# Moving the sums of the down projection's weights to another stage, and twelve additions to another engine, in a hybrid decoder layer

## The chip, the cores and the metric

The kernel runs on one core of one Trainium2 chip. The metric is the device time of one execution in microseconds; several runs are summed up by their median. The engines have short names in the profile: PE is TensorE's matrix products (PEld its weight loads), DVE is VectorE, ACT is ScalarE, POOL is GpSimd, SP is SyncE, which issues most of the transfers. Each engine takes its instructions from a queue of its own, in order: one that waits holds up those behind it.

## The reference

One layer of a hybrid decoder for 1024 tokens of width 1024, with 16 learned meta tokens in front:

```
hn = rmsnorm(h, mix_norm_g);  proj = hn @ w_in
o_sb  = stick_breaking_attention(8 heads of 64)
o_ssm = ssd_mixer(conv of 4 taps + silu, 16 heads of 64, state 128, gate, rmsnorm)
o_mla = mla_attention(8 heads of 64 + 32, low-rank q and kv)
h = h + concat(o_sb, o_ssm, o_mla) @ w_out
fn = rmsnorm(h, ffn_norm_g)
h = h + (silu(fn @ w_gate) * (fn @ w_up)) @ w_down        # width 2816
out = rmsnorm(h, final_norm_g)
```

All in float32. The kernel makes each product from three, by splitting each operand into a high part (rounded, fp32r) and a low remainder: high x high, low x high, high x low.

## The kernel before, in words

The stages follow one another in the program, and each is a block of pools: stick-breaking attention for four pairs of heads (with the convolution's dense products `conv_unit` and the next pair's projections between); the state-space chunks (`ssd_chunk`, nine of them) with the latent projections (`latent_units`, `latent`, `scaled_unit`); eight MLA heads (`mla_head`) followed in the program by the gate's products (`gate_units`) and the output projection (`out_rows`); the gate and up projections (`GateUp`); the down projection.

The order in which the instructions really stand in the queues is not the program's. The framework's scheduler puts each instruction into its engine's queue by its own model of time: those earlier in the program go first, but one that is further back is taken when its engine would be free, its inputs are there and its buffer is free. So dense products stand between the attention's steps.

A dense product takes its weights by `load_w`: a load into `wraw` (one buffer), ScalarE's cast to `whi`, POOL's remainder `wlo` (L136). TensorE's lines L147 to L149 are the three products.

The down projection, gate and up are done by a fast scheme with seven products in place of eight (Strassen in Winograd's form): of the 22 blocks of the inner width, 18 are taken as nine pairs (NS = 9). It needs sums of blocks of the weights. `down_sums(p, c)` makes those for `w_down`, pair p and column quarter c, 36 calls in all: two loads of 128 KB into a tile `wd` of 2 KB per partition (L694), four POOL operations of 128 x 128 (L696) and a store of 256 KB to `s_wsum` (L697), which the down projection reads from 1563 us on. In the kernel before, `wd` uses the buffers `vst` and `vsp` (tags of one buffer each, in pool `sbb`), which `load_value_steps` also uses for the values of the next pair of heads (loads at L408, POOL's L410 and L359). The calls stand in the loop over pairs of heads, three after each convolution unit. Other POOL work of that stage: `csig` (L496), `oTs` (L351); other loads and stores on SP: `s_osbl` (L353), `s_xs` (L497), `wraw` (L132).

POOL's work in the state-space chunks: `y` (L755), `Xd` (L802), `S` (L833), `y` plus `ea` (L825). SP's there: `bc` and `xs` (L751, L752), `lraw` (L859). In the MLA heads: POOL's `mlo` (L960), `V` (L359), and `gy` (L537), `grow` (L510) of the gate; SP's `st` (L956).

Memory: the pools concerned are stacked from the right edge of SBUF. The stick-breaking stage has sbq, sbv and sbb, with tiles for 107.4 KB per partition; the last tags that sbb holds are the buffers `oTh` and `oTl` (oTs). After it, `ga` (4.2 KB) stays, and above it `la` and `p2` (45.8 and 53.5 KB) for the state-space chunks and latents; these go, and `ml` and `mr` (44.2 and 57.3 KB) come for the MLA heads. `reuse_waits="tile"` lets a tile wait only for the tiles that lay at its place.

The down projection loops over the seven products (`product(i, banks, start)`) and in each over the nine pairs; `operands(i, p)` loads a weight block and a hidden block into `raw`, ScalarE casts (L1517), and the remainder is made in two halves, one by POOL and one by VectorE (both L1519). TensorE's products are L1529 to L1531. The first product is kept in four tiles `E1` (the tiles named grow and E in the profile), and later added to three quarters of the result `hT` (hF in the profile): twelve additions of 128 x 512 by the helper `add` (L1104), in the kernel before on POOL.

Of the kernel before, what the change touches and what calls it, by code (L numbers as in the profile page):

```python
# [11 lines left out]
F32 = mybir.dt.float32  # L12
# [3 lines left out]
ALU = mybir.AluOpType  # L16
# [19 lines left out]
NS = 9  # L36
# [23 lines left out]
def tile_hybrid_block(ctx: ExitStack, tc: tile.TileContext, a: dict):  # L60
    nc = tc.nc
    act, dve, pool, pe, sp = nc.scalar, nc.vector, nc.gpsimd, nc.tensor, nc.sync
# [24 lines left out]
    s_wsum = dram.tile([NS, 4, 128, 4, 128], F32, name="s_wsum")  # L87
# [29 lines left out]
    for e, (m, base) in enumerate(((sb_mask, -1), (mla_mask, 0))):  # L117
# [3 lines left out]
            out=full, in_=full, pattern=[[-1, 128]], compare_op=ALU.is_ge, fill=NEG,  # L121
# [139 lines left out]
    def normalise(i, row):  # L261
# [11 lines left out]
        out=tri, in_=tri, pattern=[[1, 128]], compare_op=ALU.is_ge, fill=0.0, base=0, channel_multiplier=-1  # L273
# [366 lines left out]
    for i, (q0, qn) in enumerate(((0, 256), (256, 384), (640, 384))):  # L640
# [3 lines left out]
        c0, n = CH_ALL[i]  # L644
# [8 lines left out]
    with ctx_sb as st:  # L653
        sbb = st.enter_context(tc.tile_pool(name="sbb", bufs=2, side="right", reuse_waits="tile"))
        sc = st.enter_context(tc.tile_pool(name="sc1", bufs=3, space=PSUM, reuse_waits="tile"))
        pvp = st.enter_context(tc.tile_pool(name="pv1", bufs=1, space=PSUM, reuse_waits="tile"))

        def sb_row(Qh, Kh, KSh, i):
            n_all = META + 128 * (i + 1)
            cm = sbb.tile([128, T], F32, tag="cm", bufs=4, name="cm")  # L660
            qs = Qh[:, 128 * i : 128 * (i + 1)]
            chunks = key_chunks(i)
            for c0, n in chunks[::-1]:
                ps = sc.tile([128, 512], F32, tag="sc", name="sc_ps")
# [14 lines left out]
        pms = meta_tiles(sbb)  # L679

        def sb_attend(p, proj, values):
            Q, K, KS = proj
            for h in range(2):
                for j in range(NQ // 2):
                    rows = [sb_row(Q[h], K[h], KS[h], 2 * j + e) for e in range(2)]
                    weighted_values(tp, pvp, sbb, j, rows, values[0], h, [x[p, 64 * h : 64 * (h + 1)] for x in (s_osbh, s_osbl)], pms[j % 2], values[1])

        def down_sums(p, c):

            w = sbb.tile([128, 5, 2, 64], F32, tag=("vst", "vsp")[c % 2], bufs=1, name="wd")  # L690
            w = w.rearrange("p b h d -> p (b h d)")[:, :512].rearrange("p (q n) -> p q n", q=4)
            for e in range(2):
                src = a["w_down"][2 * p + e].rearrange("p (h c n) -> p h c n", h=2, c=4)
                sp.dma_start(w[:, e::2], src[:, :, c])  # L694
            for out, x, y, op in ((2, 0, 2, ALU.subtract), (3, 3, 2, ALU.subtract), (0, 0, 3, ALU.add), (1, 1, 3, ALU.subtract)):
                pool.tensor_tensor(w[:, out], w[:, x], w[:, y], op=op)  # L696
            sp.dma_start(s_wsum[p, c], w)  # L697

        sums = [(p, c) for p in range(NS) for c in range(4)]
        values = load_value_steps(sbv, sbb, 0)  # L700
        step_sizes()
        convs = [8, 9, 10, 11, 0, 1, 2, 3, 4, 5, 6, 7]
        for p in range(4):
            sb_attend(p, proj, values)
            if p < 3:
                if p == 1:
                    sb_values(1, [load_w(a["w_sbv"][1, u]) for u in range(2)], range(9))
                proj, k_evac, q_evac = sb_project(p + 1)
                dense_fm(dpool, load_w(a["w_sbk"][p + 1]), KT, 128, hn_mov, CH_ALL, k_evac)
                dense_fm(dpool, load_w(a["w_sbq"][p + 1]), KT, 128, hn_real, CH_REAL, q_evac)  # L710
                values = load_value_steps(sbv, sbb, p + 1)
            for u in convs[3 * p : 3 * p + 3]:
                conv_unit(u)
                for x in sums[:3]:
                    down_sums(*x)
                del sums[:3]
    real = [(128 * b, 128) for b in range(NQ)]


# [221 lines left out]
    with ExitStack() as st:  # L941
        ml = st.enter_context(tc.tile_pool(name="ml", bufs=2, side="right", reuse_waits="tile"))
        mr = st.enter_context(tc.tile_pool(name="mr", bufs=2, side="right", reuse_waits="tile"))
        sc = st.enter_context(tc.tile_pool(name="sc4", bufs=3, space=PSUM, reuse_waits="tile"))
        pvp = st.enter_context(tc.tile_pool(name="pv4", bufs=1, space=PSUM, reuse_waits="tile"))

# [52 lines left out]
        def mla_head(c):  # L999
            nonlocal V  # L1000
            p, h = c // 2, c % 2
            if h == 0:
                V = load_values(mr, s_v, p, ml)
            proj = mla_load(c)
            inv = mr.tile([128, NQ], F32, tag="inv", bufs=2, name="inv")
            for j in range(NQ // 2):
                rows = [mla_row(proj, i, inv[:, i : i + 1]) for i in (2 * j, 2 * j + 1)]
                weighted_values(tp, pvp, mr, j, rows, V, h, s_omla[p, 64 * h : 64 * (h + 1)], pms[j % 2])

                if j == 1 and c == MLA_HEADS - 1:  # L1010
                    inverse_sums(c, inv, 0, NQ // 2)
            inverse_sums(c, inv, NQ // 2 if c == MLA_HEADS - 1 else 0, NQ)

        def inverse_sums(c, inv, i0, i1):
# [4 lines left out]
            dve.reciprocal(rows, pt[:n, 0:128])  # L1019
            sp.dma_start(s_inv[c, 128 * i0 : 128 * i1].rearrange("(i p) -> i p", p=128), rows)  # L1020

        V = None
        pms = meta_tiles(mr)
        for c in range(MLA_HEADS):
            mla_head(c)
        gate_r = gate_units()
        spread_row(grow, gate_r, real, CH_REAL)
        hn_stack.close()
# [74 lines left out]
    def add(out, x, y, eng=None):  # L1103
        (eng or dve).tensor_tensor(out, x, y, op=ALU.add)  # L1104
# [437 lines left out]
    gather(B, 4, lo)  # L1542
    for o in range(4):
        for ot, c in ((o, 1), (o + 4, 0), (o + 4, 1)):
            add(hT[ot][:, HALF[c]], hT[ot][:, HALF[c]], E1[o], pool)
    product(2, A, False)
    gather(A, 0, lo)
    product(5, B, False)
# [191 lines left out]
```

## Time and profile before

| what | us |
|---|---|
| median of 3 runs | 1823.75 (1821.61 to 1826.12) |
| the profiled execution's own time | 1822.58 |
| its span, first to last instruction | 1820.7 |
| TensorE busy | 1718.0 (94%), mean granted clock 0.975 |
| VectorE busy | 1101.7 (61%) |
| ScalarE busy | 849.5 (47%) |
| POOL busy | 932.1 (51%) |
| DMA | 227.08 MB, 125 GB/s on the mean |

The profile is of one execution. A row of "busy by stretch" gives the stretch from and to in us from the span's start, its length, then for each engine its busy time and its instructions in brackets, the granted TensorE clock as a share of full speed, the DMA engines' busy share and GB/s. A row of the waits reads "who waited <- for what: us in all, how often, longest". A row of a group reads "line engine operation output<-inputs shape xcount | busy us, mean ns of one | idle before it". A row of the timeline reads "start, us, engine, line ..." with the idle time before it and what ended it in square brackets. A matrix product's end is modelled, so rows of TensorE overlap; the distance between their starts is its pace.

### The profile page before, as it was taken

The numbers are of one execution on the slowest core, as the hardware profiler recorded it, in microseconds if no ns is written. First come the engines' busy times: TensorE is split into PE (matmuls) and PEld (weight loads), VectorE is DVE, ScalarE is ACT, GpSimd is POOL, SyncE is SP. The second block draws the span as 40 slices with busy tenths as digits, with TensorE's granted clock in tenths as the row PEclk, the third lists the DMA queues.
The fourth block names the chain that finished last, engine by engine and source line by source line (L and its number), as shares of the span: only waits on it lengthen the run. The fifth ranks groups of instructions, "written<-read, shape, count | busy, mean of one in ns | idle before, by whom it ended". The sixth has DMA issues, their size and how long they took to land.

```text
span 1820.7 us, 26880 instructions
## 1 busy us (share of the span) xinstructions
PE 1718.0 (94%) x9769; PEld 1504.6 (83%) x9769; DVE 1101.7 (61%) x1681; ACT 849.5 (47%) x1809; POOL 932.1 (51%) x743
## 2 busy tenths in 40 slices
PE   8959999979999988999999999899999999989997
PEld 7849998979998768998888877678888888868887
DVE  8687665657744563445675646986566676554434
ACT  7545564545557654667544423522222232343333
POOL 4446437665357646555321334655445445387643
PEclk9969999999999989999999999899999999999999
DMA  4223235443253456435631424132333322886502
GB/s 157 60 75 121 85 90 161 143 145 107 78 163 115 150 166 177 125 110 173 201 93 41 120 81 157 53 104 95 108 115 101 98 93 98 310 256 208 162 1 93
DMA packets 176456, 227.08 MB, mean 125 GB/s; under 512 B 25586, under 2 KB 121876, under 8 KB 176324
## 3 DMA queue, kind: packets, MB, share of 16 engines
q1 hardware_dynamic: 156928, 209.81, 36.7%
q10 hardware_dynamic: 19396, 15.56, 2.8%
q8 instruction: 77, 1.26, 0.3%
q14 instruction: 55, 0.45, 0.1%
HBM read 155.20 MB, written 70.12 MB: 124 GB/s over the span
## 4 chain that ended last, share of the span: by engine, by line
PE 63%; DVE 11%; POOL 7%; DMA 7%; ACT 6%; issue 5%; SPq 1%; ACTq 0%; POOLq 0%; DVEq 0%
PE d_ps L147 6%; PE b_ps L1315 6%; PE b_ps L1317 6%; PE b_ps L1316 6%; PE d_ps L148 6%; PE d_ps L149 6%; PE b_ps L1530 2%; PE b_ps L1531 2%; PE b_ps L1529 2%; POOL wd L696 2%; DMA wd<-in_w_down_dram 1%; PE ptg L322 1%; ACT L L796 1%; PE pv L301 1%; PE ptg L324 1%
## 5 line engine op out<-in xcount | busy, mean ns | idle before, releaser
L147 PE MATMUL d_ps<-hnh,whi 128*128 128x384 f32 (+6 forms) x744 | 248.7, 334 | 7.8 <-DVE cacc L491 5.4
L148 PE MATMUL d_ps<-hnh,wlo 128*128 128x384 f32 (+6 forms) x744 | 245.5, 330 | 2.1 <-POOL wlo L136 2.1
L149 PE MATMUL d_ps<-hnl,whi 128*128 128x384 f32 (+6 forms) x744 | 246.6, 331 | 0.0
L136 POOL TENSOR_TENSOR wlo<-wraw,whi 128x1024 fp32r<-128x1024 f32 (+1 forms) x57 | 136.5, 2395 | 185.1 <-ACT whi L134 166.1
L147 PEld LDWEIGHTS d_ps<-hnh,whi 128*128 128x128 f32 (+1 forms) x744 | 140.8, 189 | 12.7 <-issue 5.8
L148 PEld LDWEIGHTS d_ps<-hnh,wlo 128*128 128x128 f32 (+1 forms) x744 | 140.8, 189 | 5.5 <-POOL wlo L136 2.4
L149 PEld LDWEIGHTS d_ps<-hnl,whi 128*128 128x128 f32 (+1 forms) x744 | 140.8, 189 | 2.5 <-issue 0.3
L1315 PE MATMUL b_ps<-T,wh 128*128 128x512 f32 x352 | 138.2, 393 | 0.5 <-DVE u L1104 0.5
L1316 PE MATMUL b_ps<-T,wl 128*128 128x512 f32 x352 | 138.2, 393 | 0.0
L1317 PE MATMUL b_ps<-T,wh 128*128 128x512 f32 x352 | 137.7, 393 | 0.1
L308 DVE TENSOR_TENSOR pl<-ptg,ph 128x512 fp32r<-128x512 f32 (+1 forms) x160 | 99.3, 629 | 48.3 <-ACT ph L307 47.0
L1519 POOL TENSOR_TENSOR op<-raw,op 128x512 fp32r<-128x512 f32 x61 | 97.9, 1615 | 58.4 <-ACT op L1517 57.4
L1519 DVE TENSOR_TENSOR op<-raw,op 128x512 fp32r<-128x512 f32 x61 | 64.4, 1066 | 84.4 <-ACT op L1517 84.4
L674 DVE TENSOR_TENSOR_SCAN cm<-cm,zcol 128x144 f32<-128x144 f32 (+3 forms) x64 | 100.6, 1577 | 22.7 <-ACT cm L672 22.5
L1517 ACT CAST op<-raw 128x1024 fp32r<-128x1024 f32 x61 | 63.6, 1053 | 106.7 <-PE d_ps L1531 75.0
L696 POOL TENSOR_TENSOR wd<-wd 128x128 f32<-128x128 f32 x144 | 81.6, 581 | 61.3 <-DMA wd<-in_w_down_dram 58.2
L307 ACT CAST ph<-ptg 128x512 fp32r<-128x512 f32 (+1 forms) x160 | 84.8, 541 | 48.1 <-PE ptg L324 33.4
L1098 POOL TENSOR_TENSOR wlo<-raw,whi 128x1024 fp32r<-128x1024 f32 x18 | 45.5, 2528 | 96.6 <-ACT whi L1097 96.6
L491 DVE SCALAR_TENSOR_TENSOR cacc<-d_ps,cw,cacc 128x384 f32<-128x384 f32 (+3 forms) x108 | 61.8, 573 | 48.3 <-ACT cacc L484 46.3
L134 ACT CAST whi<-wraw 128x1024 fp32r<-128x1024 f32 (+1 forms) x57 | 58.8, 1032 | 48.2 <-PE d_ps L149 32.7
L1097 ACT CAST wh<-raw 128x512 fp32r<-128x512 f32 x88 | 52.8, 615 | 58.5 <-PE b_ps L1317 55.7
L1315 PEld LDWEIGHTS b_ps<-T,wh 128*128 128x128 f32 x352 | 66.1, 188 | 16.4 <-DVE u L1104 1.3
(443 smaller groups left out, 5311.2 us busy)
## 6 DMA issues: line engine op xcount, KB each, us to landing
s_hops<-gs SPq DMA_DIRECT2D x63, 256.0 KB, 2.0
raw<-s_hops SPq DMA_DIRECT2D x63, 256.0 KB, 5.0
raw<-in_w_gate_dram SPq DMA_DIRECT2D x22, 512.0 KB, 3.5
raw<-in_w_up_dram SPq DMA_DIRECT2D x22, 512.0 KB, 4.3
wd<-in_w_down_dram SPq DMA_DIRECT2D x72, 128.0 KB, 2.7
s_wsum<-wd SPq DMA_DIRECT2D x36, 256.0 KB, 2.6
raw<-s_wsum SPq DMA_DIRECT2D x36, 256.0 KB, 4.7
wraw<-in_w_o_dram SPq DMA_DIRECT2D x16, 512.0 KB, 4.4
```

The source lines that it names most:

```text
L136: pool.tensor_tensor(lo[:, :cols], raw[:, :cols], f32(hi[:, :cols]), op=ALU.subtract)
L147: pe.matmul(ps[:m, :n], wh, mh, start=(kt == 0), stop=False)
L148: pe.matmul(ps[:m, :n], wl, mh, start=False, stop=False)
L149: pe.matmul(ps[:m, :n], wh, ml, start=False, stop=(kt == nkt - 1))
L307: act.copy(ph[:, :n], pt[:, :n])
L308: dve.tensor_tensor(pl[:, :n], pt[:, :n], f32(ph[:, :n]), op=ALU.subtract)
L674: dve.tensor_tensor_scan(rev, rev, zcol.to_broadcast([128, n_all]), 1.0, ALU.mult, ALU.add)
L696: pool.tensor_tensor(w[:, out], w[:, x], w[:, y], op=op)
L1315: pe.matmul(banks[j], hi[:, ks], UH[u][k], start=start and k == 0, stop=False, skip_group_check=skip)
L1316: pe.matmul(banks[j], lo[:, ks], UH[u][k], start=False, stop=False, skip_group_check=skip)
L1317: pe.matmul(banks[j], hi[:, ks], UL[u][k], start=False, stop=stop and k == 3, skip_group_check=skip)
L1519: eng.tensor_tensor(lo[:, s], raw[:, s], f32(hi[:, s]), op=ALU.subtract)
```

## The change

`down_sums` and its list `sums` move from the stick-breaking stage's block to that of the MLA heads. Its tile gets a pool of its own, `wd`, with one buffer of 2 KB per partition, opened behind `ml` and `mr`. The calls stand behind the heads: six behind each of heads 1 to 6. And the twelve additions of `E1` lose the argument `pool`, so that `add` puts them on VectorE.

```
-        def down_sums(p, c):
-
-            w = sbb.tile([128, 5, 2, 64], F32, tag=("vst", "vsp")[c % 2], bufs=1, name="wd")
-            w = w.rearrange("p b h d -> p (b h d)")[:, :512].rearrange("p (q n) -> p q n", q=4)
...
-        sums = [(p, c) for p in range(NS) for c in range(4)]
...
             for u in convs[3 * p : 3 * p + 3]:
                 conv_unit(u)
-                for x in sums[:3]:
-                    down_sums(*x)
-                del sums[:3]
...
         mr = st.enter_context(tc.tile_pool(name="mr", bufs=2, side="right", reuse_waits="tile"))
+        wd = st.enter_context(tc.tile_pool(name="wd", bufs=1, side="right", reuse_waits="tile"))
...
+        def down_sums(p, c):
+
+            w = wd.tile([128, 4, 128], F32, tag="wd", bufs=1, name="wd")
+            for e in range(2):
+                src = a["w_down"][2 * p + e].rearrange("p (h c n) -> p h c n", h=2, c=4)
+                sp.dma_start(w[:, e::2], src[:, :, c])
+            for out, x, y, op in ((2, 0, 2, ALU.subtract), (3, 3, 2, ALU.subtract), (0, 0, 3, ALU.add), (1, 1, 3, ALU.subtract)):
+                pool.tensor_tensor(w[:, out], w[:, x], w[:, y], op=op)
+            sp.dma_start(s_wsum[p, c], w)
...
+        sums = [(p, c) for p in range(NS) for c in range(4)]
         for c in range(MLA_HEADS):
             mla_head(c)
+            for x in sums[:6] if c > 0 else ():
+                down_sums(*x)
+                sums.remove(x)
...
     for o in range(4):
         for ot, c in ((o, 1), (o + 4, 0), (o + 4, 1)):
-            add(hT[ot][:, HALF[c]], hT[ot][:, HALF[c]], E1[o], pool)
+            add(hT[ot][:, HALF[c]], hT[ot][:, HALF[c]], E1[o])
```

More of the change, by code (lines that the diff above doesn't have):

```diff
@@ L686, in sb_attend @@
                     weighted_values(tp, pvp, sbb, j, rows, values[0], h, [x[p, 64 * h : 64 * (h + 1)] for x in (s_osbh, s_osbl)], pms[j % 2], values[1])
-        def down_sums(p, c):
-            w = sbb.tile([128, 5, 2, 64], F32, tag=("vst", "vsp")[c % 2], bufs=1, name="wd")
-            w = w.rearrange("p b h d -> p (b h d)")[:, :512].rearrange("p (q n) -> p q n", q=4)
[L692 to L697, printed above, removed]
-        sums = [(p, c) for p in range(NS) for c in range(4)]
         values = load_value_steps(sbv, sbb, 0)
```

## The prediction

> **What bounds the kernel now.** I read the page's busy times first, then busy time by stretch, then the waits and the chain inside the stretches that the change touches.
>
> ```profile
> PE 1718.0 (94%) x9769; PEld 1504.6 (83%) x9769; DVE 1101.7 (61%) x1681; ACT 849.5 (47%) x1809; POOL 932.1 (51%) x743
> ...
> L696 POOL TENSOR_TENSOR wd<-wd 128x128 f32<-128x128 f32 x144 | 81.6, 581 | 61.3 <-DMA wd<-in_w_down_dram 58.2
> ```
>
> ```profile
> core 0: us, PE busy (x) PEld busy (x) DVE busy (x) ACT busy (x) POOL busy (x), PEclk, DMA share, GB/s
> ...
> 512.00:700.00 188.00, 177.07 (x1268) 150.09 (x1267) 104.24 (x180) 112.71 (x316) 111.50 (x79) 0.97 0.49 152
> 700.00:830.00 130.00, 124.21 (x858) 120.33 (x857) 57.14 (x139) 88.67 (x218) 77.12 (x61) 1.00 0.45 130
> ...
> 140.00:260.00 120.00, 119.97 (x880) 115.95 (x880) 83.15 (x113) 69.91 (x165) 52.74 (x57) 1.00 0.31 93
> 300.00:420.00 120.00, 104.27 (x664) 98.86 (x663) 68.94 (x103) 56.47 (x128) 85.25 (x114) 0.97 0.48 150
> 1598.00:1640.00 42.00, 35.58 (x143) 28.50 (x142) 24.40 (x21) 19.18 (x22) 39.52 (x26) 0.92 0.79 249
> ```
>
> ```profile
> 360.00:400.00 40.00, 29.42 (x182) 27.07 (x181) 20.91 (x30) 17.04 (x39) 26.52 (x38) 0.95 0.43 135
> ```
>
> TensorE bounds the program: 94% busy, 102.7 us idle in the whole span, so an edit is worth only the idle (and the slowed clock) that it takes away or puts in. The rows show where. In 140 to 260, in the stick-breaking stage, TensorE never stops. In 300 to 420, the same stage with most of the sums in it, it idles 15.7 us and its clock is at 0.97; 360 to 400 alone holds 10.6 us of that. In 1598 to 1640, the start of the down projection, it idles 6.4 us at clock 0.92 while POOL is full (39.5 of 42). The state-space stage, 512 to 700, has 10.9 us idle, and POOL busy for 59% of it.
>
> The chain of waits, cut to 265 to 420, and the waits of 355 to 425 say what stands in front of TensorE there:
>
> ```profile
> by line: POOL wd L696 18.6%; DMA wd<-in_w_down_dram 17.1%; DMA s_wsum<-wd 13.0%; issue 8.1%; POOL wlo L136 7.0%; DMA vsp<-s_vsb 4.1%; PE d_ps L147 3.6%; POOL csig L496 3.6%; PE d_ps L148 3.4%; PE d_ps L149 3.4%; POOL vst L410 2.7%; DMA wraw
> ```
>
> ```profile
> POOL wd L696 <- DMA wd<-in_w_down_dram: 23.9, 12, 4.9
> ...
> ACT cacc L484 <- DMA wraw<-in_w_xbc_dram: 9.1, 1, 9.1
> ACT Q L605 <- DMA wraw<-in_w_xbc_dram: 8.3, 1, 8.3
> ...
> PE d_ps L148 <- POOL wlo L136: 2.1, 1, 2.1
> ```
>
> Nearly half of that chain (18.6 + 17.1 + 13.0%) is the sums: load, four POOL operations, store, next load. They stand in POOL's and SyncE's queues in front of what TensorE needs, the weights' remainders (wlo, L136) and the next weights' load (wraw); ScalarE twice waits 8 to 9 us for that load.
>
> **The change part by part.** First, the sums leave the stick-breaking stage: 144 POOL operations, and on SyncE 72 loads and 36 stores.
>
> ```profile
> L696 POOL TENSOR_TENSOR wd<-wd x144: 446/460/2581, 123.0 to 417.9; 128x128 f32<-128x128 f32 x144
> L694 SPq DMA_DIRECT2D wd<-in_w_down_dram x72: 540/583/1480, 120.3 to 413.7; - x72
> L697 SPq DMA_DIRECT2D s_wsum<-wd x36: 319/326/543, 125.5 to 418.3; - x36
> ```
>
> ```profile
> wd<-in_w_down_dram SPq DMA_DIRECT2D x72, 128.0 KB, 2.7
> s_wsum<-wd SPq DMA_DIRECT2D x36, 256.0 KB, 2.6
> ```
>
> That is 81.6 us of POOL work, 58.2 us in which POOL stands waiting for their loads, and 72 x 0.583 + 36 x 0.326 = 54 us of SyncE's issuing.
>
> ```profile
> L696 POOL TENSOR_TENSOR wd<-wd x36: 452/460/2581, 123.0 to 179.4; 128x128 f32<-128x128 f32 x36
> ```
>
> The nine earliest sums (36 operations, in 123 to 180) cost nothing: 140 to 260 is full, with most of them inside. The others stand in 265 to 420. The top of the gain is all idle of 300 to 420 and the slowed clock: 15.7 + 0.03 x 104 = 18.9 us. The bottom is the one TensorE wait there that names POOL's wlo, 2.1 us. I take what 360 to 400 shows, 10.6 + 0.05 x 29 = **12 us**, because there the two waits for wraw stand; the rest of 300 to 420 I leave where it is, since projections and the value loads (vst, vsp) change over there too.
>
> Second, where they go. The loop emits them behind heads 1 to 6 of the MLA stage, but it emits and does not place: an instruction runs when its engine is free and its buffer too.
>
> ```profile
> 115.93 0.36 SPq L408 DMA_DIRECT2D vst<-s_vsb  x1
> 120.29 1.26 SPq L694 DMA_DIRECT2D wd<-in_w_down_dram  x2
> ```
>
> ```profile
> 481.05 0.53 SPq L1034 DMA_DIRECT2D gssm<-in_ssm_g_dram  x1
> ...
> 509.72 0.46 SPq L353 DMA_DIRECT2D s_osbl<-oTs  x1
> ```
>
> The first sum's load went out right behind the last load into the tag that it shares, long before the convolution that it is written behind; gssm, written behind the MLA heads, was loaded at 481. So the new buffer's place decides. Counted from the right edge by the tiles' sizes, ga, la and p2 reach 103.5 KB, ga, ml and mr 105.7 KB, and the new 2 KB lie behind those: in what the stick-breaking pools (107.4 KB) held last, the buffers oTs, whose last store is issued at 509.7. I expect the sums from about 512, in the state-space stage. With one buffer a sum takes an issue, a landing, four operations and a store's landing: 0.6 + 2.7 + 4 x 0.46 + 0.3 + 2.6 = 8 us, so 24 by 700 and the last at about 800. The waiting store and load on SyncE have behind them the loads bc and xs (L751, L752), lraw, wraw and, from 700, st; those are issued a buffer ahead, which covers a wait of some us, and costs as much as the wait if it is gone.
>
> What a sum costs there is POOL's queue: 4 x 0.58 + 58.2/36 = 3.9 us each, waits included. The chain in 512 to 700:
>
> ```profile
> by line: ACT L L796 11.2%; issue 7.2%; PE d_ps L147 7.1%; PE d_ps L148 6.9%; ACT ea L793 6.8%; PE d_ps L149 6.6%; POOL y L825 4.7%; PE yd L820 4.4%; POOL S L833 4.2%; DVE L L811 4.1%; DMA s_y<-y 3.7%; PE sps L829 3.5%; POOL y L755 3.4%; PE
> ```
>
> POOL carries 4.7 + 4.2 + 3.4 = 12.3% of it, so I charge 24 x 3.9 x 0.123 = **11.5 us**. The other 12 sums, in the heads, I cost at nothing: POOL has 53 us free in 700 to 830 against 12 x 3.9 = 47, and 140 to 260 is a stretch of the same kind (attention with dense work between) where sums cost nothing. Bounds: nothing at all, as there; and the price of the old place for all, 18.9 / 27 x 36 = 25 us. 11.5 lies between because POOL is on this stage's chain but does not lead it. The DMA engines (share 0.49) cover 24 x 0.5 MB in 188 us, 67 GB/s more beside 152.
>
> Third, twelve additions of the kept product (hF<-hF,grow and hF<-hF,E, L1104) go from POOL to VectorE.
>
> ```profile
> L1104 DVE TENSOR_TENSOR T<-T,hT 128x512 f32<-128x512 f32 x4 | 2.6, 681 | 0.0
> ```
>
> ```profile
> L1104 POOL TENSOR_TENSOR hF<-hF,E 128x512 f32<-128x512 f32 x6 | 10.3, 1729 | 0.0
> L1104 POOL TENSOR_TENSOR hF<-hF,grow 128x512 f32<-128x512 f32 x6 | 9.4, 1591 | 0.0
> L1104 POOL TENSOR_TENSOR tt<-tt 128x512 f32<-128x512 f32 x4 | 5.2, 1290 | 10.3 <-ACT tt L1602 10.3
> ```
>
> ```profile
> 1605.67 13.62 DVE L1519 TENSOR_TENSOR op<-raw,op 128x512 fp32r<-128x512 f32 x8 [1.18 <-ACT op L1517]
> ```
>
> ```profile
> 1610.27 1.73 POOL L1519 TENSOR_TENSOR op<-raw,op 128x512 fp32r<-128x512 f32 x1
> 1611.95 6.79 POOL L1104 TENSOR_TENSOR hF<-hF,E 128x512 f32<-128x512 f32 x4
> 1618.70 13.77 POOL L1519 TENSOR_TENSOR op<-raw,op 128x512 fp32r<-128x512 f32 x10
> ```
>
> ```profile
> 1621.68 0.80 PE L1530 MATMUL b_ps<-op 128*128 128x512 f32 x1 [5.71 <-POOL op L1519]
> 1622.28 0.63 PE L1531 MATMUL b_ps<-op 128*128 128x512 f32 x1
> ...
> 1627.82 0.43 PE L1530 MATMUL b_ps<-op 128*128 128x512 f32 x1
> 1628.09 0.39 PE L1531 MATMUL b_ps<-op 128*128 128x512 f32 x1
> 1628.32 0.40 PE L1530 MATMUL b_ps<-op 128*128 128x512 f32 x1
> ```
>
> Four additions (6.8 us) stand on POOL in front of the remainder that TensorE waits for, 5.71 us at 1621.68; then 14 products to 1627.82 take 6.1 us where 14 x 0.23 = 3.2 is normal, 2.9 us more at a lower clock. With the 0.7 us wait before it, this place costs 6.4 + 2.9 = 9.3 us. With the additions gone POOL's next remainder starts 6.8 us earlier. VectorE is late next: it splits the other half of each operand, and with POOL running its op takes 13.62 / 8 = 1.70 us where one alone takes 0.68. Between 1598.7 and 1632.5 POOL did 14 splits and 8 additions; if pairs keep 1.70 and the additions take 0.68 on VectorE, 14 x 1.70 + 8 x 0.68 = 29.3 us replace 33.8, which is 4.5 us, and most of the slowed clock goes with the long stall. I take **7 us**; bounds 9.3 (all) and nothing (the wait only changes engines). The last four additions, behind the gather at 1636, have a TensorE without idle around them: nothing.
>
> The Trainium skill ("SBUF — State Buffer", section "SBUF: two separate sides") says that a VectorE operation with two inputs in SBUF and a GpSimd operation that reads it hold one port pair exclusively, the later one waiting the whole instruction out; this speaks against the move. The trace agrees in part: 1.70 us per pair, against 0.68 + 1.29 = 1.97 by an exclusive lock. By the lock the 36 operations would take 22 x 1.29 + 14 x 0.68 = 37.9 us before and 14 x 1.29 + 22 x 0.68 = 33.0 after, a gain of 4.9 us, and the sum below would end 2 us higher.
>
> Sum against the profiled execution's own 1822.58 us (span 1820.7 and 1.9 around it): 1822.6 - 12 - 7 + 11.5 = 1815.1. The median of the three runs, 1823.75, stands 1.2 above that execution, so I predict **1816 us**, 0.4% faster; its own range is 1810 to 1818. A change of 0.3%, 5.5 us, is about what a measurement of this kernel can tell from none.
>
> **The rivals.** *Free ride:* the state-space stage hides the sums, or the buffer becomes free only with the MLA heads, at 700 or later, where TensorE leads and POOL has room. For it: POOL's 76 us idle in 512 to 700. Against: its share of the chain. Then -12 to -19 and -7 remain: about 1802.
>
> *Even:* the gain of the one stage is paid in the other, or VectorE takes over POOL's wait at 1621. For it: 1.70 us beside POOL. -12 - 7 with 18 to 19 for the sums, or -12 and 11.5 alone: about 1822 to 1824.
>
> *Slower:* POOL becomes the bound of the state-space stage. 111.5 + 24 x 3.9 = 205 us do not fit in 188. The stage grows by that 17 us, and by those of POOL's present pauses that no sum can fill, since an early load's landing holds the queue: of 76 us I put a fifth, 15. It decides from where a sum's four operations wait for their load in order in front of y (L825) or S (L833). Then -19 + 32: about 1836. Against: sums stand in POOL's queue only where it was free.
>
> That the additions stay on POOL, or the sums in their stage, the code excludes.
>
> **How the numbers follow.** Forecast 0.40 (1810 to 1818), free ride 0.20 (1799 to 1807), even 0.20 (1819 to 1828), slower 0.20 (1829 to 1840). The range 1799 to 1831 leaves out most of the slower case and the lower tail, under 2 in 10. Faster 0.60, same 0.20, slower 0.20 are these cases.
>
> **What would show it.** Right: no wd in 100 to 420, TensorE's idle in the stretch up to there down from 15.7 to under 6; wd starting near 500 and running to about 800; L825 and L833 with longer waits before them and the state-space stage 10 us longer; TensorE's wait at the first products under 2 us with L1104 hF on VectorE at 0.7 to 1.7 us. Wrong: wd first seen after 690; the waits for wraw (9.1, 8.3) still there; TensorE waiting for VectorE's op at the same place; a stage between 512 and 700 that grows by over 20 us or not at all.

## The result and the profile after

The change made the kernel slower. The median went from 1823.75 us (1819.38 to 1826.12, 13 runs) to 1832.57 us (1824.92 to 1842.93, 13 runs); the ratio that is given here and below, taken from all runs and not from the two medians, is 1.0056, with a 95% interval of 1.0037 to 1.0075. The forecast was 1816. The profiled execution of the changed kernel took 1840.2 us (span 1838.4), at the high end of its runs, against 1822.58 (span 1820.7) of the one before, so stage differences between these two add up to 17.7 us of span where the medians differ by 8.8. The same sums in the run e1_sums_only below took 1831.0 us in its profiled execution, and show the same stages growing.

In the changed kernel the pool `wd` and the moved lines shift the numbers: the sums are L1013 (loads), L1015 (POOL) and L1016 (store); y (L825 before) is L810, ea L778, the scores' first product L965.

The page of the kernel after, busy times and the group of the sums:

```profile
PE 1733.7 (94%) x9769; PEld 1518.2 (83%) x9769; DVE 1113.0 (61%) x1693; ACT 853.7 (46%) x1809; POOL 912.9 (50%) x731
...
L1015 POOL TENSOR_TENSOR wd<-wd 128x128 f32<-128x128 f32 x144 | 69.9, 496 | 66.6 <-DMA wd<-in_w_down_dram 62.2
```

Busy time by stretch, first of the kernel before, then of the kernel after. The stretches are the chunks' stage (from the first product of the chunks, R, to the first score product of the heads) and the heads' stage (from there to the first product L1198 of the last rows, at 1072.7 before and 1088.7 after). The rows' very first product, L1197, stands 0.2 us ahead of that before and 3.2 after, with other dense products between; so some 3 of the 25 us below are a matter of order at this border.

```profile
517.00:709.00 192.00, 180.07 (x1280) 153.05 (x1280) 99.86 (x178) 115.35 (x322) 113.73 (x82) 0.97 0.49 152
709.00:1072.00 363.00, 352.73 (x2211) 319.81 (x2212) 204.44 (x431) 204.65 (x495) 146.43 (x96) 1.00 0.40 120
```

```profile
300.00:420.00 120.00, 119.93 (x798) 116.34 (x797) 89.89 (x124) 67.99 (x149) 49.16 (x34) 1.00 0.22 67
...
499.00:700.00 201.00, 186.74 (x1297) 159.14 (x1297) 98.28 (x178) 118.79 (x325) 146.42 (x149) 0.96 0.61 190
700.00:1088.00 388.00, 364.08 (x2195) 328.55 (x2194) 209.79 (x434) 204.56 (x492) 180.68 (x175) 0.96 0.46 139
```

In 300 to 420 TensorE's idle went from 15.7 us to 0.1 and its clock from 0.97 to 1.00. The chunks' stage grew by 9 us. The heads' stage grew by 25: its idle went from 10.3 to 23.9 us, and its clock from 1.00 to 0.96, which over 364 us of work is another 14 or so (an estimate from these two rows). Of the 23.9 us, 18.0 stand in 700 to 912, while the sums run. POOL is busy for 181 of the stage's 388 us, 47%.

POOL's operations of the sums in two stretches (busy, count) and the tile's own rows, kernel after:

```profile
490.00:700.00 210.00, 32.22 (x65) 0.96 0.63 193
700.00:920.00 220.00, 37.69 (x79) 0.95 0.61 186
```

```profile
L1015 POOL TENSOR_TENSOR wd<-wd x144: 444/459/1455, 505.2 to 911.4; 128x128 f32<-128x128 f32 x144
```

They start near 500, as expected, but 16 sums stand in the chunks' stage and 20 in the heads', where 24 and 12 were expected, and the last ends at 912, not 800. A sum took (912 - 498) / 36 = 11.5 us of the one buffer, not 8. The chain of waits of the kernel after, cut to 700 to 865:

```profile
by line: DMA s_wsum<-wd 22.5%; DMA wd<-in_w_down_dram 22.3%; POOL wd L1015 12.5%; issue 6.7%; POOL wlo L136 4.3%; SPq L1013 3.1%; DMA wraw<-in_w_z_dram 2.6%; POOL gy L537 2.4%; DMA st<-s_qr 1.9%; PE d_ps L147 1.6%; POOL mlo L946 1.5%; PE d_
```

Store, next load, POOL's operations: 57% of the chain in this cut (24% over 700 to 1090), more than the 49% that the same ring held in 265 to 420 before. So the ring heads the chain of waits here as it did there. The waits of the kernel after in 490 to 920 on SyncE's queue and, for all engines, in 690 to 1090 show the two queues that the ring holds:

```profile
SPq L1016 <- POOL wd L1015: 64.0, 29, 6.5
SPq L1013 <- DMA s_wsum<-wd: 60.8, 30, 6.4
SPq L1016 <- DMA wd<-in_w_down_dram: 21.6, 17, 3.7
```

```profile
POOL wd L1015 <- DMA wd<-in_w_down_dram: 50.5, 25, 8.6
DVE go L539 <- POOL gy L537: 38.8, 18, 6.4
```

SyncE stood 146 us for the ring in 490 to 920, POOL 50 us for its loads in 690 to 1090. The gate's `go` waits 38.8 us for POOL (26.8 before). One such place, from the timelines of the kernel after in 785 to 797:

```profile
789.78 0.46 POOL L1015 TENSOR_TENSOR wd<-wd 128x128 f32<-128x128 f32 x1 [4.98 <-DMA wd<-in_w_down_dram]
...
795.00 0.72 POOL L537 TENSOR_TENSOR gy<-gy,gs 128x256 f32<-128x256 f32 x1
795.07 0.62 ACT L356 CAST V<-vst 16x128 fp32r<-16x128 f32 x2 [5.42 <-POOL V L372]
795.75 0.42 DVE L539 TENSOR_TENSOR go<-d_ps,gy 128x256 f32<-128x256 f32 x1 [5.57 <-POOL gy L537]
796.45 0.45 PE L965 MATMUL sc_ps<-mhi 96*128 96x384 f32 x1 [2.52 <-ACT pr L980]
```

POOL stands 4.98 us for a sum's load, with `V` and the gate's `gy` behind it; VectorE and ScalarE stand over 5 us for those two, and ScalarE's next exponentials, for which TensorE waits, come after. So here the sums reach TensorE through POOL's queue.

The down projection kept its time. TensorE's waits of the kernel after in 1590 to 1665, and the timelines of TensorE, VectorE and POOL there:

```profile
PE b_ps L1531 <- DVE op L1519: 6.5, 2, 6.0
```

```profile
1638.35 0.79 PE L1531 MATMUL b_ps<-op 128*128 128x512 f32 x1 [6.00 <-DVE op L1519]
```

```profile
1620.66 6.91 DVE L1104 TENSOR_TENSOR hF<-hF,grow 128x512 f32<-128x512 f32 x4
1627.50 1.78 DVE L1519 TENSOR_TENSOR op<-raw,op 128x512 fp32r<-128x512 f32 x1
1629.21 6.82 DVE L1104 TENSOR_TENSOR hF<-hF,E 128x512 f32<-128x512 f32 x4
```

```profile
1616.68 20.46 POOL L1519 TENSOR_TENSOR op<-raw,op 128x512 fp32r<-128x512 f32 x12 [11.65 <-ACT op L1517]
```

The wait of 5.71 us for POOL became one of 6.00 us for VectorE. Four additions stand in front of VectorE's split as they had stood in front of POOL's. An addition takes 6.91 / 4 = 1.73 us on VectorE while POOL splits at 20.46 / 12 = 1.71 us beside it, as long as on POOL before (1.73).

The stages of all runs in us, from the timelines of one profiled execution each: the start of the chunks' first product; then the lengths of the chunks' stage, the heads' stage, the rows and the feed-forward products up to the first product of the down projection, and the rest; and the span.

| run | start of chunks | chunks | heads | up to down | down to end | span |
|---|---|---|---|---|---|---|
| before | 517.4 | 192.1 | 363.2 | 504.7 | 243.3 | 1820.7 |
| after | 499.7 | 201.0 | 388.0 | 506.6 | 243.1 | 1838.4 |
| e1_sums_only | 501.6 | 197.8 | 382.3 | 504.3 | 243.1 | 1829.1 |
| e2_adds_only | 520.5 | 192.5 | 365.1 | 505.8 | 242.4 | 1826.3 |
| e3_dma_only | 500.1 | 215.3 | 366.7 | 505.9 | 241.5 | 1829.5 |
| e4_no_ring | 494.5 | 200.1 | 364.8 | 503.0 | 243.5 | 1805.9 |
| e5_no_adds | 515.2 | 194.4 | 364.6 | 504.1 | 233.4 | 1811.7 |
| e6_ffn | 500.5 | 188.1 | 364.6 | 535.9 | 245.1 | 1834.2 |
| e7_gated | 498.1 | 188.6 | 391.5 | 509.8 | 241.6 | 1829.6 |
| e8_adds_late | 514.7 | 191.3 | 365.1 | 506.2 | 241.4 | 1818.7 |
| e9_gated_dma | 500.3 | 186.2 | 386.9 | 505.9 | 242.0 | 1821.3 |
| e10_gated_free | 502.1 | 189.1 | 383.6 | 505.3 | 241.4 | 1821.5 |
| e11_adds_spread | 513.9 | 192.1 | 365.3 | 504.7 | 233.5 | 1809.5 |
| e12_sb_spread | 549.5 | 178.5 | 353.8 | 511.5 | 241.4 | 1834.7 |
| e13_early | 525.6 | 190.9 | 363.8 | 505.3 | 233.5 | 1819.1 |
| e14_chunks | 500.0 | 211.0 | 367.7 | 511.3 | 233.4 | 1823.4 |
| e15_split | 503.5 | 198.1 | 366.6 | 500.7 | 233.4 | 1802.3 |

Rows without a sum in a stage show its floor: about 500 for the start, 363 to 368 for the heads, 503 to 507 up to the down projection, and a tail of 233.4 without the burst of additions. The chunks have two: 191 to 194 where sums stood in the stage ahead of them, as before, and 186 to 189 where none did; differences "above the floor" below are against the second. e12 (shorter chunks and heads behind a late start) and what e7, e12, e14 and e15 show up to the down projection lie outside of these. Five runs whose code is the same up to there (before, e2, e5, e8, e11) start the chunks anywhere from 513.9 to 520.5, so a difference of a few us in one stage says nothing alone.

### The profile page after: what moved, and what is told of

It is laid out like the page before. It is cut to its first block, busy times and chain, and to the rows that moved or that the text cites. A ratio compares the mean times of both kernels' runs of the same rounds, so it can differ in the third digit from the quotient of the medians.

```text
span 1838.4 us, 26867 instructions
## 1 busy us (share of the span) xinstructions
PE 1733.7 (94%) x9769; PEld 1518.2 (83%) x9769; DVE 1113.0 (61%) x1693; ACT 853.7 (46%) x1809; POOL 912.9 (50%) x731
## 4 chain that ended last, share of the span: by engine, by line
PE 57%; DMA 13%; DVE 12%; POOL 6%; ACT 5%; issue 5%; SPq 1%; ACTq 0%; POOLq 0%; DVEq 0%
PE b_ps L1315 6%; PE b_ps L1316 6%; PE b_ps L1317 6%; PE d_ps L147 6%; PE d_ps L148 6%; PE d_ps L149 6%; DMA s_wsum<-wd 3%; DMA wd<-in_w_down_dram 3%; PE b_ps L1531 2%; PE b_ps L1529 2%; PE b_ps L1530 2%; POOL wd L1015 2%; PE ptg L322 1%; DVE cm L674 1%; PE ptg L324 1%
## 5 line engine op out<-in xcount | busy, mean ns | idle before, releaser
L1519 POOL TENSOR_TENSOR op<-raw,op 128x512 fp32r<-128x512 f32 x61 | 101.7, 1676 | 73.2 <-ACT op L1517 71.7
L674 DVE TENSOR_TENSOR_SCAN cm<-cm,zcol 128x144 f32<-128x144 f32 (+3 forms) x64 | 104.1, 1637 | 18.9 <-ACT cm L672 18.5
L1015 POOL TENSOR_TENSOR wd<-wd 128x128 f32<-128x128 f32 x144 | 69.9, 496 | 66.6 <-DMA wd<-in_w_down_dram 62.2
L1519 DVE TENSOR_TENSOR op<-raw,op 128x512 fp32r<-128x512 f32 x61 | 54.4, 901 | 76.8 <-ACT op L1517 76.8
L496 POOL TENSOR_TENSOR csig<-csig,cacc 128x384 f32<-128x384 f32 (+1 forms) x36 | 45.0, 1249 | 73.2 <-ACT csig L495 44.3
```

The source lines that it names most:

```text
L1519: eng.tensor_tensor(lo[:, s], raw[:, s], f32(hi[:, s]), op=ALU.subtract)
```

## The experiments

**The two parts alone: e1_sums_only and e2_adds_only.** The first is the kernel after with

```
-            add(hT[ot][:, HALF[c]], hT[ot][:, HALF[c]], E1[o])
+            add(hT[ot][:, HALF[c]], hT[ot][:, HALF[c]], E1[o], pool)
```

and the second is the kernel before with the reverse of that line.

> The sums moved, the twelve additions still on POOL. Theory (the sums' ring of load, four operations, store, next load stands in POOL's and SP's queues in the MLA stage, and the additions do nothing): slower than before by all of the 9 us, 1829 to 1838, first product of the last rows near 1088, PE's stall at the start of the down projection still named by POOL. Rival (the additions on VectorE cost as well): 1824 to 1828.

Measured: 1833.01 us, ratio 1.0051 (1.0035 to 1.0068); the theory's range held.

> The additions on VectorE, the sums where they were before. Theory (each addition beside POOL takes 1.7 us on VectorE as it did on POOL, the stall only changes engines): within 0.15% of before, 1821 to 1827, PE waiting some 6 us for VectorE's op. Rival (it is a gain that the moved sums hide): 1815 to 1818. Rival (it is a loss): 1828 or more.

Measured: 1824.56 us, ratio 1.0012 (0.9997 to 1.0027). TensorE again waits 6.0 us for VectorE's `op`. The sums carry the whole loss, and the additions' move is worth nothing that these runs can tell.

**Which half of a sum costs: e3_dma_only and e4_no_ring.** Both have the additions on POOL. e3 leaves the four POOL operations out. e4 sends the weights straight to the store, and POOL works on constants:

```
-            for out, x, y, op in (...):
-                pool.tensor_tensor(w[:, out], w[:, x], w[:, y], op=op)
```

```
-                sp.dma_start(w[:, e::2], src[:, :, c])
+                sp.dma_start(s_wsum[p, c][:, e::2], src[:, :, c])
...
-                pool.tensor_tensor(w[:, out], w[:, x], w[:, y], op=op)
-            sp.dma_start(s_wsum[p, c], w)
+                pool.tensor_tensor(w[:, out], ones, ones, op=op)
```

> As e1, but the four POOL operations of each sum are left out: the blocks are loaded into wd and stored as they are (the sums are not made, so the output is not the reference's). The ring of transfers and SP's 108 issues stay, POOL's 144 operations and its waits go. Theory A (POOL's queue, standing for the sums' loads, delays gy, grow and wlo): the loss of the state-space and MLA stages goes, 1803 to 1811. Theory B (SP's queue, standing for the store, delays the loads behind it): stays slower, 1824 to 1836.

Measured: 1829.97 us, ratio 1.0039 (1.0018 to 1.0059). Theory B. Without POOL's operations all 36 rings ran from 499 to 758, most of them in the chunks' stage, which grew by 23 us over before.

> As e1, but the ring is taken apart: the same bytes go from w_down to s_wsum in 72 transfers within DRAM, and POOL's 144 operations of the same size work on resident constants and wait for no transfer (the sums are not made). The amount of POOL work and of bytes stays, the waiting goes. Theory (the waiting for loads in order is the price): 1803 to 1812. Rival (the amount of POOL work is the price, 70 to 80 us in stages where POOL is on the chain): 1818 to 1832.

Measured: 1807.93 us, ratio 0.992 (0.9897 to 0.9943), as the theory had it. But the run takes away more than the waiting: bound to no buffer, the transfers went out at the start of the program:

```profile
L1013 SPq DMA_DIRECT2D s_wsum<-in_w_down_dram x72: 490/605/1531, 19.0 to 91.7; - x72
```

POOL's work stood in 487 to 673, all of it ahead of the heads, without a transfer beside it. The chunks' stage was 12 us above its floor, and the heads' stage, with no sum in it, at its own. So the ring of transfers alone loses nearly as much as the whole sums (1829.97 against 1833.01), and POOL's operations alone cost the chunks 12 us where the ring cost 27 above the floor. On the heads e4 says nothing.

**The additions: e5_no_adds, e8_adds_late, e11_adds_spread.** All are the kernel before with the twelve additions left out (e5), put on POOL behind its last remainder of the second product (e8), or spread (e11):

```
+    E1_TO = {2: [(o + 4, 1) for o in range(4)], 5: [(o, 1) for o in range(4)], 7: [(o + 4, 0) for o in range(4)]}
...
+            if i in E1_TO and p % 2 == 1:
+                o = p // 2
+                ot, c = E1_TO[i][o]
+                eng = (pool, dve)[o % 2]
+                with tc.issue_after(last_on(mybir.EngineType.Pool)), tc.issue_after(last_on(DVE)):
+                    add(hT[ot][:, HALF[c]], hT[ot][:, HALF[c]], E1[o], eng)
```

> The kernel before without the twelve additions of the kept product (part of the result is missing). Theory (the additions in the operands' queue make the stall, whichever engine has it): the 6 us wait and the slowed clock behind it go, 1812 to 1818. Rival (the stall comes from the operands' late loads, 13 us without one, and the additions only fill the time): 1821 to 1826.

Measured: 1813.56 us, ratio 0.9947 (0.9928 to 0.9966); the theory held.

> The kernel before with the twelve additions on POOL held behind the last POOL remainder of the second product. Theory (they cost because they stand in front of remainders while the operands have no lead): the first stall goes, 1813 to 1819. Rival (it comes back a product later at the same size): 1821 to 1827.

Measured: 1821.76 us, ratio 0.9998 (0.9986 to 1.0011). The rival held: TensorE's wait, 5.9 us, comes back at a later operand.

> The kernel before with one edit: the twelve additions of the kept product are spread, one behind every second pair's operands in products 2, 5 and 7 in place of four at once behind a product, alternating between POOL and VectorE. Theory (the 9.7 us that leaving the additions out is worth are a burst of 4 x 1.7 us in front of the next operand; operands are made about a pair ahead, so one addition of 1.7 us is covered): no TensorE wait of over 2 us at the first products, 1813 to 1817 us. Rival (the operands' pace itself is what POOL and VectorE hold, so that each addition costs its time wherever it stands): 1819 to 1824, with many TensorE waits of about 1 us.

Measured: 1812.98 us, ratio 0.9947 (0.9929 to 0.9965), the same as without additions: all twelve cost nothing, as the theory had it. TensorE's waits of e11_adds_spread in 1570 to 1810, and the additions there:

```profile
PE d_ps L176 <- POOL rl L1624: 2.9, 1, 2.9
```

```profile
L1104 POOL TENSOR_TENSOR hF<-hF,grow x3: 1289/1295/1736, 1616.2 to 1661.1; 128x512 f32<-128x512 f32 x3
L1104 DVE TENSOR_TENSOR hF<-hF,grow x3: 1774/1778/1789, 1618.4 to 1665.3; 128x512 f32<-128x512 f32 x3
```

The only wait left belongs to the end of the program and stands in e5 too. On VectorE an addition is no shorter, 1.78 us; on POOL two of these three took 1.29. One at a time, they fit into the lead that the operands have. What cost 9.7 us was four in a row on one engine, and it cost as much on VectorE (e2) as on POOL. This run spreads the additions and alternates the engines at once; which of the two would do alone was not run.

**Another stage: e6_ffn.** The kernel after, additions on POOL, with the sums beside the gate and up projections, four behind each of nine pairs, in the buffers of that stage (`w = q_tile("wd")`).

> The sums made beside the gate and up projections, in the buffers of 2 KB that stand there (ten of them), four behind each of nine units; the additions on POOL. Theory (a sum costs only where its waiting stands in front of what TensorE needs next; in that stage TensorE is full, POOL half busy, and the weights are prefetched): the stick-breaking stage's gain stays and nothing is paid, 1800 to 1810. Rival (POOL's work there, wl of L1098, is as tight and pays): 1815 to 1830.

Measured: 1837.74 us, ratio 1.01 (1.0068 to 1.0133). Chunks and heads are at their floors, and the part up to the down projection takes 535.9 us, 31 more. That is slower than the rival too. The longest row of TensorE's waits of e6 in 1100 to 1700 is one that the kernel before does not have there:

```profile
PE b_ps L1300 <- ACT wh L1082: 21.0, 8, 3.7
```

ScalarE's casts of the next weights come late. What holds them up was not followed further.

**Inside the heads' stage: e7_gated, e9_gated_dma, e10_gated_free.** All with the additions on POOL, and the sums held in their place behind each head:

```
+            with tc.issue_after(last_on(SP)):
                 for x in sums[:6] if c > 0 else ():
```

e9 has no POOL operations; e10 is e4's form, held behind POOL's last instruction too.

> As e1, but SP takes a sum's loads only behind the last SP instruction of the head it is written behind, so that no sum stands in the state-space stage. Theory (both stages pay for the ring): the state-space stage is back at before's 168 us, the heads and what follows pay more, 1822 to 1835. Rival (the state-space stage is what costs): 1805 to 1815.

Measured: 1834.69 us, ratio 1.0073 (1.0046 to 1.01). The theory's range held; the sums ran from 780 to 1094.

> Against the kernel with the sums gated behind the heads (1834.69 us, heads' stage 391.5 us where 363.2 is the kernel before's), this one leaves out the 144 POOL operations (the stored sums are unsummed weights); the 72 loads, 36 stores and their ring in one buffer stay, behind the same heads; the additions stand on POOL as before. Theory A (in the heads' stage the cost is POOL standing in order in front of a sum's load): no POOL operation waits, so the stage falls to 363 to 369 us and the kernel to 1804 to 1813. Theory B (the cost is SyncE standing in the ring in front of the heads' own loads and stores): the stage stays at 380 us or more, the kernel at 1823 to 1836.

Measured: 1826.19 us, ratio 1.0018 (1.0003 to 1.0034). Theory B.

> The same place behind the heads, but the ring is gone: 72 transfers go straight from the weights to the sums' store, and the 144 POOL operations work on constants, so that none waits for a load (the sums aren't made). POOL's work alone, 36 x 1.9 = 70 us, stands among the heads. Theory A (POOL's waiting for loads is the cost, its work is not): the heads' stage 363 to 370 us, the kernel 1804 to 1813. Theory C (POOL's work itself is too much for the heads' stage): the stage 378 us or more, 1820 or more. Theory B (SyncE's ring) expects as theory A here, 1804 to 1813.

Measured: 1819.2 us, ratio 0.9981 (0.9966 to 0.9996). POOL's waits for the sums in e7 in 690 to 1090, then the heads' stage by stretch in e7, e9 and e10:

```profile
POOL wd L1015 <- DMA wd<-in_w_down_dram: 111.4, 51, 7.7
```

```profile
687.00:1078.00 391.00, 367.00 (x2222) 331.79 (x2222) 202.23 (x429) 203.40 (x492) 207.55 (x231) 0.96 0.51 156
```

```profile
687.00:1073.00 386.00, 364.94 (x2208) 330.07 (x2207) 202.24 (x430) 204.55 (x494) 146.81 (x95) 0.96 0.53 161
```

```profile
691.00:1075.00 384.00, 364.82 (x2213) 328.93 (x2213) 205.98 (x435) 205.96 (x498) 203.14 (x241) 0.97 0.47 139
```

The heads' stage grew by 28 us with both, by 24 with the ring alone, and by 20 with POOL's work and 72 direct transfers, POOL being 53% busy and never waiting for a load. Theory A (POOL's waiting alone) fell for this place: with it, and POOL's work too, taken away, 24 of 28 remained.

How the ring alone reaches TensorE, e9's timelines show. SyncE's waits in 778 to 1060, and its queue, VectorE and TensorE around the largest loss (927 to 947: 6.9 us idle, clock 0.78):

```profile
SPq L1014 <- DMA wd<-in_w_down_dram: 61.3, 37, 5.0
SPq L1013 <- DMA s_wsum<-wd: 47.1, 27, 3.9
```

```profile
928.73 1.20 SPq L1013 DMA_DIRECT2D wd<-in_w_down_dram  x2
931.98 0.33 SPq L1014 DMA_DIRECT2D s_wsum<-wd  x1
932.35 0.43 SPq L1051 DMA_DIRECT2D xraw<-s_ossm  x1
```

```profile
936.24 1.23 DVE L1052 TENSOR_TENSOR xraw<-xraw,grow 128x1024 f32<-128x1024 f32 x1 [7.41 <-DMA xraw<-s_ossm]
937.39 0.55 DVE L308 TENSOR_TENSOR pl<-ptg,ph 128x384 fp32r<-128x384 f32 x1
937.99 0.37 PE L301 MATMUL pv<-pl,V 128*64 128x128 f32 x1 [5.07 <-DVE pl L308]
```

SyncE stands 108 us for the ring's own landings. Here a load of the output projection, `xraw`, is queued behind the ring's store, which waits for the ring's load; VectorE stands 7.41 us for `xraw`, with the heads' `pl` behind it in its queue, and TensorE waits 5.07 us for `pl`. VectorE's waits for `xraw<-s_ossm` in 690 to 1095 are 20.5 us in e7 and 12.4 in e9, but 1.2 in the kernel before, 0.7 in the one after and 1.3 in e10. In the kernel after the sums end at 912, ahead of these loads, and the place at 790 goes through POOL's queue. So the same ring was paid in different queues, by what stood behind it.

The 20 us of e10 are less clear. Half of them stand in one place, in 1051 to 1071:

```profile
1051.00:1071.00 20.00, 13.70 (x49) 10.75 (x48) 7.67 (x9) 3.50 (x5) 7.03 (x3) 0.74 0.19 54
```

```profile
1057.80 0.80 PE L147 MATMUL d_ps<-raw,whi 128*128 128x512 f32 x1 [6.30 <-DVE hT L1076]
```

That is 6.3 us of idle and 0.26 x 13.7 = 3.6 of slowed clock (an estimate from the row), over 160 us behind the last of e10's POOL operations for the sums (887) and over 60 behind the last of its direct transfers (984). Its profiled execution is also the slowest of its ten runs, 4 us above their median. So e10 does not show that POOL's work alone costs the heads 20 us. The scheduler orders each variant anew (the last exponential of the heads stands at 999 us in e10, at 1048 before), and how much of each loss is order and how much is waiting was not separated.

**Does the old stage have cover: e12_sb_spread, e13_early.** e12 is the kernel before with the last 18 sums at the end of the stick-breaking stage. e13 has the spread additions, and all sums behind the first six of the twelve convolution units, which is their first half:

```
-                for x in sums[:3]:
+                for x in sums[:6]:
```

> The kernel before with one edit: the first 18 sums stay behind the first two thirds of the convolution's products, none stands in the third, and the last 18 come behind SyncE's last instruction of the stage's last convolution products, still in the shared buffers. Theory (the sums cost the stick-breaking stage 12 to 19 us because they stand in front of the weights' loads and remainders of 300 to 420, and cost nothing where the stage has cover): the idle of 300 to 420 falls from 15.7 us to under 6 and the kernel to 1808 to 1816. Rival (they spill into the state-space stage, or the stage's end has no cover either): 1818 to 1828, TensorE's idle found again between 420 and 540.

Measured: 1835.41 us, ratio 1.0066 (1.0044 to 1.0089). The sums ran to 542, and the chunks began 32 us later, of which the next two stages gave back 23. The rival had the place; its time, 1818 to 1828, was exceeded.

> The kernel with the spread additions (1812.98 us), and all 36 sums in the first two thirds of the stick-breaking stage, six behind each convolution unit in place of three, in the same two shared buffers. It tells whether that part has cover, as the prediction argued from 140 to 260. Theory (sums cost nothing where attention and dense work leave TensorE full, and cost something only in 300 to 420): the idle of 300 to 420 falls from 15.7 us to under 7, none comes in 140 to 260, 1798 to 1805 us. Rival (a ring of loads, POOL operations and stores costs 0.3 to 0.7 us of TensorE a sum in any stage, and more where it is denser): idle of 8 us or more appears in 140 to 260, 1809 to 1825.

Measured: 1822.84 us, ratio 1.0008 (0.9996 to 1.0021), 10 us slower than e11; the rival held. Busy time by stretch of e13:

```profile
140.00:260.00 120.00, 111.56 (x775) 105.89 (x774) 74.78 (x104) 61.24 (x146) 68.69 (x90) 0.96 0.40 123
...
300.00:420.00 120.00, 108.48 (x680) 103.19 (x679) 75.88 (x107) 58.41 (x131) 73.58 (x88) 0.94 0.41 124
```

In 140 to 260, where six sums (24 POOL operations) had stood beside a TensorE without idle, fifteen (60 operations) put in 8.4 us of idle and take 4% of the clock. The cover of that stretch ends between the two.

**All beside the chunks, or half: e14_chunks, e15_split.** Both have the spread additions; the sums have a pool of two buffers in the chunks' stage, four behind each chunk (e14), or two, with the first 18 left in their old place (e15). Lines of e15:

```
-                for x in sums[:3]:
+                for x in sums[:3] if p < 2 else ():
...
+        wd = p2_st.enter_context(tc.tile_pool(name="wd", bufs=2, side="right", reuse_waits="tile"))
...
             ssd_chunk(c)
+            for x in sums[:2]:
+                down_sums(*x)
```

> The kernel with the spread additions, and the sums behind the state-space chunks, four behind each of the nine, in a pool of their own with two buffers; none stands beside the heads. Theory (the heads' stage paid 19 to 25 us and the state-space stage about 9 for two thirds of the sums; with two buffers the load of the next sum lands while this one is added up): stick-breaking -19, state-space stage +9 to +13, heads 363 to 367: 1801 to 1807 us. Rival (the stage that takes all 36 pays for all, 0.7 us each, as it did in the run with the transfers alone, +23): 1811 to 1820.

Measured: 1828.82 us, ratio 1.0038 (1.0021 to 1.0055). The rival had the stage right and the time too low (1811 to 1820): POOL waits only 17.1 us for the loads, yet the chunks' stage takes 211 us, 23 above its floor. Another 7 come up to the down projection, unexplained.

> The kernel with the spread additions, the first 18 sums where they were (three behind each of the first six convolution units), the other 18 behind the state-space chunks, two behind each, in a pool of two buffers. Theory (the first 18 are covered, 18 spread over the chunks cost about half of what two thirds in one buffer cost there, 4 to 6 us): stick-breaking -10 to -15, 1801 to 1807 us. Rival (the first 18 keep the stick-breaking stage's price): stick-breaking -5 or less, 1811 to 1818.

Measured: 1805.5 us, ratio 0.9907 (0.989 to 0.9925), inside the theory's range and the fastest of those that leave nothing out: 0.9% under the kernel before and 27 us under the median of the one after. The spread additions give 0.5% of it (e11). The sums give the rest, 7.2 us of span against e11, which differs in nothing else: the chunks start 10.4 us earlier, their stage is 6.0 longer and the heads' 1.3; another 4.0 come up to the down projection, where nothing was changed, and stay unexplained. Busy time by stretch of e15_split where the sums were thinned out:

```profile
140.00:260.00 120.00, 119.84 (x882) 116.09 (x881) 83.73 (x116) 70.64 (x166) 54.40 (x58) 1.00 0.31 93
...
300.00:420.00 120.00, 113.93 (x724) 109.35 (x723) 81.11 (x115) 63.70 (x141) 55.86 (x47) 0.97 0.26 79
```

## Why the prediction was wrong

**The step that failed: the sums beside the heads, costed at nothing.** That stage grew by 25 us (19 in e1). Both arguments for zero were unsound. "POOL has 53 us free in 700 to 830 against 12 x 3.9 = 47" counts an engine's idle total, but a queue is served in order: at 789.78 POOL stood 4.98 us for a sum's load, and VectorE and ScalarE over 5 us for what was queued behind it. And the likeness to 140 to 260, "where sums cost nothing", carried over from a stretch that held 24 operations, six sums; e13 shows that the same stretch pays from some number between six and fifteen. SyncE's loads were said to be "issued a buffer ahead, which covers a wait of some us"; held beside the later heads (e9), the ring alone costs 24 us.

**The count that fed it.** The cycle of 8 us was worked out as if each step were issued at once. In the queues it was 11.5, so 20 sums and not 12 came to the heads. How much of the 25 us the eight more account for no run shows.

**The additions, forecast -7, measured nothing** (-0.2 in the two profiles; e2 is 2 us slower with an interval that includes zero). The failed term is "the additions take 0.68 on VectorE": those in front of TensorE's wait took 1.73 beside POOL's splits. The lower bound, "the wait only changes engines", is what happened, step for step: 5.71 us for POOL became 6.00 us for VectorE. The price of the place, 9.3 us, was right (9.7 in e5), but it belongs to the burst, which the edit left whole. The Trainium skill's rule ("SBUF — State Buffer", section "SBUF: two separate sides"), that of two such instructions the later one waits the whole of the earlier one out, was set against the row in the prediction, where by it the sum would have ended 2 us higher. The trace agrees with it more closely than the prediction said; four rows of the kernel after:

```profile
1603.19 0.69 DVE L1519 TENSOR_TENSOR op<-raw,op 128x512 fp32r<-128x512 f32 x1 [4.56 <-ACT op L1517]
1603.24 1.80 POOL L1519 TENSOR_TENSOR op<-raw,op 128x512 fp32r<-128x512 f32 x1 [9.07 <-ACT op L1517]
```

```profile
1652.82 1.29 POOL L1519 TENSOR_TENSOR op<-raw,op 128x512 fp32r<-128x512 f32 x1 [0.89 <-ACT op L1517]
...
1652.97 1.68 DVE L1519 TENSOR_TENSOR op<-raw,op 128x512 fp32r<-128x512 f32 x1
```

The first of a pair takes its time alone (0.69, 1.29). The second ends 1.16 us behind the first on POOL and 0.54 on VectorE; these add up to 1.70, the pace side by side (1.71 and 1.73). The 1.97 of the prediction added whole lengths. What its working by the rule left out is the queue: it counted what both engines need in all, but TensorE waited for a split of VectorE with four additions in front of it, each taking its turn with POOL.

**The gain in the stick-breaking stage, forecast -12, was -17.7 in the profiles** (517.4 to 499.7) and -15.8 in e1, inside the bounds of 2.1 and 18.9: the idle of all of 300 to 420 went, so the upper bound's row was the one to take. **The chunks' stage, forecast +11.5, was +9** (+5.7 in e1). That it came so near is luck in part: it holds 16 sums and not 24. It shows the wait that was expected, with ScalarE's `ea` waiting 35.6 us for POOL's y where it was 25.1. So the sum that the runs give is -17.7 + 8.9 + 24.8 and 1.7 for the rest, which is the 17.7 us by which the spans differ.

**The rivals.** The slower one had the right sign and nearly the time (1836), but the wrong place, so that its time is luck: it put 32 us into the chunks' stage, which paid 9. "Even" had the additions' part exactly.

## What to carry to other kernels

The free time of an engine does not price work that is put into it. A ring of load, operations and store can be paid in each in-order queue that it shares, so look at what stands behind each of its waits. A stretch that hides a few does not hide many, and one that hides them is no evidence for another. Here it paid to spread such work over two stages (18 and 18, 7 us better than 36 in the best single place). When a wait comes from a burst, try splitting the burst before changing its engine.

## What the runs showed of the hardware

An addition of 128 x 512 that takes 0.68 us alone on VectorE took 1.73 to 1.78 us beside POOL, as long as on POOL itself (1.73). Of two such fp32 operations, one on each engine, the one that starts second waits the first out (1.80 us for 1.29 on POOL, 1.68 for 0.69 on VectorE). Moving the twelve additions from one of the two queues to the other gained no time.

TensorE's loss comes about double: in the heads' stage, five runs with 19 to 24 us of scattered idle (after, e1, e7, e9, e10) had a granted clock of 0.96 to 0.97, and the other twelve, with 4 to 14, one of 0.98 to 1.00. In the kernel after, 13.6 us of new idle came with about as much slowed work.
